# First transfers in another order, and the first norm's weights spread by TensorE

## The chip, the cores and the metric

The kernel runs on one core of one Trainium2 chip. The metric is the device time of one execution in microseconds (us), the median of several runs. The engines are named as the profile names them: PE is TensorE (matrix products), DVE is VectorE, ACT is ScalarE, POOL is GpSimd, SP is SyncE, which here only issues transfers (DMAs).

## The reference

One decoder layer over 1024 tokens of width 1024, all float32. What matters for this case is its first step; the rest is sketched.

```python
def rmsnorm(x, w):
    xf = x.astype(jnp.float32)
    y = xf * lax.rsqrt(jnp.mean(xf * xf, axis=-1, keepdims=True) + NORM_EPS)
    return (y * w.astype(jnp.float32)).astype(x.dtype)
...
    u = rmsnorm(h, norm1_w[l])                       # (1024, 1024), the first step
    proj = jnp.einsum('bsd,de->bse', u, w_in[l])     # 1024 x 3584
    ...
    ya = dilated_attention_group(qa, ka, va)         # 8 heads of 64, three window patterns
    yb = hgrn2_group(qb, fb, ib, gb, lb_table[l], hgrn_norm_w[l])   # 4 heads, gated recurrence
    h = h + jnp.einsum('bse,ed->bsd', mixed, w_out[l])
    u2 = rmsnorm(h, norm2_w[l])
    ...                                              # SwiGLU of width 2816, residual
    return rmsnorm(h, final_norm_w)
```

## The kernel before

The 1024 tokens are eight row tiles x0 to x7 of 128 rows, two to a buffer (`xb`, printed as `E`: x0 and x1, x2 and x3, and so on). Each tile goes through `norm_rows`: ACT squares it and sums each row (L337), DVE makes the mean (`msa`, L314), POOL raises it to the power -0.5 (`rsa`, L373), and DVE multiplies each half of 512 columns by `rsa` and by the norm's weights (L305, one SCALAR_TENSOR_TENSOR for each half). The weights `w1b` are two buffers of 128x512, `wh7` and `wl7`, in which each of the 128 rows holds the same 512 numbers: `norm1_w` is one row in memory, and a transfer with a step of zero (`bcast`) writes it 128 times.

Then `blocks` transposes the normed tile u on PE against the identity (`ident`, itself a transfer; four 128x128 transposes fill a bank `b` of PSUM, L286), and splits each bank into a rounded part (`hi`, ACT, L347) and a remainder (`lo`, DVE, L301), both fp32r, so that a product in full precision is three matmuls in fp32r: a triple. The input projection runs by a Strassen scheme: a 2x2 arrangement of blocks with seven products. Tiles 0 to 3 give the right operands 1 and 2 directly; for tiles 4 to 7 the first transpose is made by true fp32 matmuls with `ident` (L280), so that the sums of the scheme can be accumulated onto it. While the tiles come in, the first products of the scheme are begun with what is there ("leads": `F0` and `K1` in halves of 256 columns first, then two more in 512). The weights of each lead come through two staging buffers `st`.

After the projections the four recurrent heads (`hgrn`), the eight attention heads and the output projection follow. The attention stage takes a row maximum (`mx`, L1011), exponentials, transposes of the probabilities (L1048) and products; the output projection's matmuls stand between them where its inputs are ready. The feed-forward network takes the second half of the span.

What sets the order: the whole kernel is recorded as a list of operations (`P.op`, `P.flex`) with their dependencies, costs and a class `P.cls`. `Prog.schedule` then plays it through with these costs and takes, for each engine as it comes free, the ready operation of the lowest class, and within a class that with the longest way to the end. Operations recorded with `P.flex` can go to one of several engines (DVE, POOL, ACT), and the planner picks. Each engine works through its own list in the order so found, and waits where an operand is not ready. A changed dependency or cost anywhere can thus move instructions far behind it. All transfers are issued by SP, in its order, into one hardware queue. Constants that the recurrent heads need (`consts`: a mask `lm`, small tables `lg` and `hw`, an exponential on ACT) are recorded after the eighth tile, in the same class 2 as the rest.

Of the kernel before, what the change touches and what calls it, by code (L numbers as in the profile page):

```python
# [13 lines left out]
AF = mybir.ActivationFunctionType  # L14
# [5 lines left out]
S = 1024  # L20
D = 1024
# [225 lines left out]
def hymba_block(ctx: ExitStack, tc: tile.TileContext, x, norm1_w, w_in, lb_logits, hgrn_norm_w, w_out,  # L247
                norm2_w, w_gate_up, w_down, final_norm_w, cos, sin, amask, lmask, eye, out):
    nc = tc.nc
    x = x[0]  # L250
# [6 lines left out]
    P = Prog()  # L257
# [5 lines left out]
    def moved(nbytes, run):  # L263

        return nbytes / run * (0.008 + run / 27e3) / 16

    def dma(o, i, nbytes, run=2048):
        r = [i] if isinstance(i, (View, Buf)) else []
        w = [o] if isinstance(o, (View, Buf)) else []
        gi = i if r else (lambda: i)  # L270
        go = o if w else (lambda: o)
        P.op("SP", 0.5, lambda: nc.sync.dma_start(go(), gi()), r, w, nbytes=moved(nbytes, run))

    def mm(items, r, w):
        cost = sum(4 * n / 2400.0 + 0.008 if f32 else n / 2400.0 + (0.0132 if n > 128 else 0.007)
                   for o, lt, rh, st, sp, n, m, f32 in items)

        def fn():
            for o, lt, rh, st, sp, n, m, f32 in items:
                nc.tensor.matmul(o(), lt(), rh(), start=st, stop=sp, skip_group_check=True)  # L280
        P.op("PE", cost, fn, r, w)
# [73 lines left out]
    whole = lambda b: b.v(lambda t: t)  # L355

    def bcast(w, n):
        return bass.AP(tensor=w.tensor, offset=w.offset, ap=[[0, 128], [1, n]])


    ident = P.buf("ident", [128, 128])
# [15 lines left out]
    def norm_rows(xt, wb, o, scr, tag):  # L377
        ss = P.buf("ss" + tag, [128, 1])
        act(scr, xt, AF.Square, D, accum=whole(ss))
        r = rstd_of(ss, 1, D, tag)  # L380
        if not isinstance(wb, list):
            stt(o, xt, whole(r), wb, OP.mult, OP.mult, D)
            return
        for i, w in enumerate(wb):
            ov, xv = (v.buf.v(lambda b, v=v, i=i: v.get(b)[:, i * 512:i * 512 + 512], v.key + (i,)) for v in (o, xt))
            stt(ov, xv, whole(r), w, OP.mult, OP.mult, 512)
# [3 lines left out]
    def bank(stream, shape=(128, 512)):  # L390
        names = BANKS[stream]
        while True:
            n = rot[stream] = rot.get(stream, -1) + 1
            tag = f"b{names[n % len(names)]}"
            if tag not in held:
                return P.buf(tag, list(shape), F32, "ps")
# [25 lines left out]
    i_d = P.buf("i_d", [S, 512], F32, "dr")  # L422
    g_d = P.buf("g_d", [512, S], F32, "dr")
    f_d = P.buf("f_d", [512, S], F32, "dr")
    q_d = P.buf("q_d", [512, S], F32, "dr")
# [5 lines left out]
    def slot(tag):  # L431
        return whole(P.buf(tag, [128, 512]))
# [125 lines left out]
    def begin(R, w, rot, stream, p1, nw=8, cut=False):  # L558

        a = halves(True, w, rot)  # L560
        L = {}
        split(L, 1, a[0, 0], nw=nw, rot=rot, heng=LEADHI, leng=LEADLO)
        split(L, 2, a[0, 1], nw=nw, rot=rot, heng=LEADHI, leng=LEADLO)
        pa = bank(stream)
        held.add(pa.tag)
        if not cut:
            product(R, pa, L, 1, True, True)
            act(p1, whole(pa), AF.Copy, 512)
            product(R, pa, L, 2, False, True)
            yield pa, p1  # L570
            return
        for c in range(2):
            piece(R, pa, L, 1, True, True, c)
            act(colv(p1.buf, c * 256, 256, c),
                colv(pa, c * 256, 256, c), AF.Copy, 256)
            piece(R, pa, L, 2, False, True, c)
            yield pa, p1
# [49 lines left out]
    def consts():  # L627
        dma(lm, lmask, 128 * 640 * 4)
        for r in range(2):
            dma(tiny.v(lambda t, r=r: t[:, 4 * r:4 * r + 4]),  # L630
                bass.AP(tensor=lb_logits.tensor, offset=lb_logits.offset + r * 512, ap=[[1, 128], [128, 4]]), 2048)
        dma(hw, bass.AP(tensor=hgrn_norm_w.tensor, offset=hgrn_norm_w.offset, ap=[[1, 128], [128, 4]]), 2048)
        c = [tiny.v(lambda t, i=i: t[:, 4 * i:4 * i + 4]) for i in range(8)]
        tt("DVE", c[2], c[0], c[1], OP.max, 4)
        for r in range(2):
            tt("DVE", c[r], c[r], c[2], OP.subtract, 4)
        act(tiny.v(lambda t: t[:, 12:20]), tiny.v(lambda t: t[:, 0:8]), AF.Exp, 8)
        tt("DVE", c[2], c[3], c[4], OP.add, 4)
        P.op("DVE", 0.1, lambda: nc.vector.reciprocal(c[2](), c[2]()), [tiny], [tiny])
        tt("DVE", c[5], c[3], c[2], OP.mult, 4)  # L640
        ts("DVE", c[6], c[5], -1.0, 1.0, 4)
# [10 lines left out]
    def src_of(w):  # L652
        c = COL[w[0]] + int(w[1]) * 256
        return w_in_v[:, :, c:c + 256], w[0] in "QK"
# [3 lines left out]
    cut = []  # L658
    for t in range(NT):
        if t == 0:  # L660
            for i in range(4):
                dma(xs[i], x[i * 128:(i + 1) * 128, :], 128 * D * 4, 4096)
                if i == 0:
                    for k in range(2):
                        dma(w1b[k], bcast(norm1_w[:, k * 512:k * 512 + 512], 512), 128 * 512 * 4)
                    dma(ident, eye, 65536)
        if t == 2:
            for i in range(4, NT):
                dma(xs[i], x[i * 128:(i + 1) * 128, :], 128 * D * 4, 4096)
        xt = xs[t]  # L670
        u = us[t % 2]
        norm_rows(xt, w1b, u, u, "a")
        blocks(t, u, R, "n", tmp4)
        if t == 0:
            hi("ACT", whole(plus), whole(ident), 128)
            ts("POOL", whole(minus), whole(ident), -1.0, 0.0, 128)
        if t == 1:
            for w in seq[:CUT[0]]:
                cut.append(begin(R, *src_of(w), "d", slot(T8[4 + len(cut)]), 7, True))
                leads[w] = next(cut[-1])  # L680
        if t == 3:
            for g in cut:
                next(g)
        if t >= 3 and len(leads) < LEAD:
            w = seq[len(leads)]
            leads[w] = next(begin(R, *src_of(w), "d", slot(T8[4 + len(leads)]), 7))
    consts()

    csn = E(16, [128, 2048])
    for v, c0 in ((cos, 0), (sin, 1)):  # L690
# [133 lines left out]
    def hgrn(h):  # L824
# [16 lines left out]

        def blocked(v, w):
            return sub(v, lambda a: a.rearrange("p c (b e) -> p c b e", e=w))
        dma(f, f_d.v(lambda b: b[rs, :], h), 128 * S * 4)
        dma(qc(0, 128), q_d.v(lambda b: b[rs, :].rearrange("p (c e) -> p c e", e=128), h), 128 * S * 4, 512)
        dma(r128(iv), i_d.v(lambda b: b.rearrange("(c p) n -> p c n", p=128)[:, :, rs], h // 2), 128 * S * 4, 512)

        def scores(n, g):

# [87 lines left out]
                rd += [half(qp, c // 4), half(ks, (c - 1) // 4)]  # L937
            mm(it, rd, [o])
        gt = A
        dma(gt, g_d.v(lambda b: b[rs, :], h), 128 * S * 4)  # L940
        ss = P.buf("hss", [128, NT])
        for g in range(2):
            yg = half(iv, g)
# [435 lines left out]
```

## Time and profile before

| | us |
|---|---|
| median of 3 runs | 1258.24 (1257.98 to 1258.44) |
| profiled execution, its own time | 1256.03 |
| span of the profiled execution, first to last instruction | 1254.2 |
| PE busy within the span | 1212.3 |
| DVE busy | 1028.3 |
| ACT busy | 476.9 |
| POOL busy | 112.0 |

The page gives busy time, not need: PE is busy for 97% of the span, and 1254.2 - 1212.3 = 41.9 us are left in which it does nothing. The profiled execution is one run; it took 1256.03 us, 1.8 us more than its span, and 2.2 us less than the median.

The columns of the timeline are: start in us, duration in us, engine, line, operation, what it writes <- what it reads, its shape and count, and in brackets how long the engine had been idle before it and what it had waited for. Buffer numbers are left out, so `E` stands for many buffers.

### The profile page before, as it was taken

How to read it: one execution, taken by the hardware profiler on the slowest of the kernel's cores; microseconds unless marked ns; L12 is line 12 of the kernel's file. 1: busy time of each engine (PE TensorE's matmuls, PEld its weight loads, DVE VectorE, ACT ScalarE, POOL GpSimd, SP SyncE). 2: the span in 40 equal slices, each digit the busy share in tenths (PEclk: the TensorE clock that was granted, in tenths of full speed). 3: DMA queues.
4: the chain of work that ended last, by engine and by line, in shares of the span. 5: the costliest groups of instructions: out<-in, count | busy, mean ns of one | idle time of the engine just before them, and what ended most of it. 6: DMA issues, size and time to landing. Idle time of an engine off the chain costs nothing.

```text
span 1254.2 us, 17960 instructions
## 1 busy us (share of the span) xinstructions
PE 1212.3 (97%) x6244; PEld 1030.7 (82%) x6244; DVE 1028.3 (82%) x2110; ACT 476.9 (38%) x1020; POOL 112.0 (9%) x212
## 2 busy tenths in 40 slices
PE   4999999999998899999999999999999999999997
PEld 4878889888987788987888888888888887888885
DVE  6999989999789999966888676676676769968986
ACT  5642332344327887842722132221222223223222
POOL 1110000101003433420100000000000000000001
PEclk9999999999999999999999999999999999999998
DMA  8434443514468753316223322323322369434433
GB/s 264 133 127 160 176 147 101 182 68 160 132 195 272 203 143 88 93 54 199 79 76 126 118 97 89 126 85 109 126 84 101 112 230 386 170 101 127 135 109 118
DMA packets 132890, 175.57 MB, mean 140 GB/s; under 512 B 18496, under 2 KB 85696, under 8 KB 132800
## 3 DMA queue, kind: packets, MB, share of 16 engines
q1 hardware_dynamic: 132800, 174.43, 42.4%
q8 instruction: 49, 0.80, 0.3%
q14 instruction: 41, 0.34, 0.1%
HBM read 122.76 MB, written 51.64 MB: 139 GB/s over the span
## 4 chain that ended last, share of the span: by engine, by line
PE 78%; DVE 9%; DMA 7%; ACT 2%; issue 1%; SPq 0%; POOL 0%; DVEq 0%; POOLq 0%; ACTq 0%
PE b L280 76%; DVE wl L301 2%; DVE E L301 2%; PE b L1048 2%; DMA st<-in_w_in_dram 1%; DVE E L864 1%; DVE wh L301 1%; PE b L286 1%; DMA m_d<-lm 1%; DMA st<-in_w_out_dram 1%; DMA E<-kl_d 1%; DVE E L305 1%; DMA i_d<-wl 1%; DVE st L301 1%; ACT wh L337 1%
## 5 line engine op out<-in xcount | busy, mean ns | idle before, releaser
L280 PE MATMUL b<-E,wh 128*128 128x512 f32 (+1 forms) x2096 | 643.6, 389 | 5.1 <-ACT wl L337 1.9
L280 PEld LDWEIGHTS b<-E,wh 128*128 128x128 f32 x2096 | 386.3, 188 | 85.5 <-DVE E L301 4.0
L280 PE MATMUL b<-E,wl 128*128 128x512 f32 (+1 forms) x1048 | 403.9, 385 | 0.0
L347 ACT ACTIVATE wh<-st 128x512 fp32r<-128x512 f32 (+1 forms) x207 | 129.4, 629 | 384.6 <-PE b L280 217.1
L301 DVE TENSOR_TENSOR wl<-st,wh 128x512 fp32r<-128x512 f32 (+1 forms) x340 | 229.5, 685 | 5.3 <-ACT wh L347 2.1
L280 PEld LDWEIGHTS b<-E,wl 128*128 128x128 f32 x1048 | 197.1, 188 | 40.7
L301 DVE TENSOR_TENSOR E<-b,E 128x512 f32<-128x512 f32 (+1 forms) x157 | 105.5, 683 | 39.6 <-PE b L280 37.3
L349 DVE TENSOR_SCALAR wh<-st 128x512 fp32r<-128x512 f32 x119 | 50.0, 423 | 88.0 <-PE b L280 84.6
L280 PE MATMUL b<-wl,wh 128*128 128x512 f32 x308 | 119.9, 389 | 0.5 <-DVE wl L301 0.5
L280 PE MATMUL b<-wh,wl 128*128 128x512 f32 x308 | 119.9, 389 | 0.1
L280 PE MATMUL b<-wh,wh 128*128 128x512 f32 x308 | 119.8, 389 | 0.0
L280 PE MATMUL b<-wl,E 128*128 128x256 f32 (+1 forms) x544 | 116.3, 287 | 2.7 <-DVE wl L301 2.6
L301 DVE TENSOR_TENSOR wl<-b,wl 128x512 f32<-128x512 f32 (+2 forms) x139 | 89.6, 651 | 14.8 <-PE b L280 12.2
L280 PE MATMUL b<-E,E 128*128 128x192 f32 (+3 forms) x464 | 99.6, 324 | 2.0 <-DVE E L305 1.0
L301 DVE TENSOR_TENSOR st<-st 128x512 f32<-128x512 f32 x136 | 92.5, 684 | 0.7
L280 PEld LDWEIGHTS b<-wl,E 128*128 128x128 f32 x544 | 88.0, 191 | 5.8 <-DVE wl L301 3.4
L337 ACT ACTIVATE E<-E 128x512 f32<-128x512 f32 (+2 forms) x77 | 54.2, 704 | 93.5 <-DVE E L301 42.5
L280 PE MATMUL b<-wh,E 128*128 128x256 f32 x448 | 89.1, 290 | 0.2 <-DVE wh L301 0.2
L280 PEld LDWEIGHTS b<-E,E 128*128 128x128 f32 x464 | 75.0, 192 | 8.0 <-issue 2.6
L349 POOL TENSOR_SCALAR wh<-st 128x512 fp32r<-128x512 f32 (+1 forms) x16 | 11.1, 692 | 747.6 <-PE b L280 668.3
L280 PEld LDWEIGHTS b<-wh,E 128*128 128x128 f32 x448 | 72.4, 192 | 0.8 <-DVE wh L301 0.4
L280 PEld LDWEIGHTS b<-wl,wh 128*128 128x128 f32 x308 | 57.8, 188 | 13.0 <-DVE wl L301 0.9
(140 smaller groups left out, 1391.7 us busy)
## 6 DMA issues: line engine op xcount, KB each, us to landing
st<-in_w_gate_up_dram SPq DMA_DIRECT2D x22, 1024.0 KB, 5.2
st<-a_d SPq DMA_DIRECT2D x77, 256.0 KB, 2.8
st<-in_w_in_dram SPq DMA_DIRECT2D x16, 1024.0 KB, 5.7
a_d<-E SPq DMA_DIRECT2D x45, 256.0 KB, 2.1
E<-in_w_down_dram SPq DMA_DIRECT2D x44, 256.0 KB, 5.3
E<-in_x_dram SPq DMA_DIRECT2D x8, 512.0 KB, 9.1
E<-qs_d SPq DMA_DIRECT2D x32, 128.0 KB, 3.9
E<-kh_d SPq DMA_DIRECT2D x32, 128.0 KB, 3.6
```

What stands on the lines that cost most here:

```text
L280: nc.tensor.matmul(o(), lt(), rh(), start=st, stop=sp, skip_group_check=True)
L286: nc.tensor.transpose(ov(), iv(), ident())
L301: P.flex(alts, lambda e: ENG[e].tensor_tensor(o(), a(), b(), op=op), [a, b], [o])
L305: lambda e: nc.vector.scalar_tensor_tensor(o(), a(), s(), b(), op0=op0, op1=op1), [a, s, b], [o])
L337: nc.scalar.activation(o(), a(), func, **kw)
L347: nc.scalar.activation(o(), i(), AF.Copy)
L349: ENG[e].tensor_scalar(o(), i(), 1.0, 0.0, op0=OP.mult, op1=OP.add)
L864: nc.vector.copy_predicated(Av, mv, ps()[:, :, a:a + 64].rearrange("p c (b e) -> p c b e", e=w))
L1048: nc.tensor.transpose(ov(), iv(), ident())
```

## The change

The first transfers are issued in another order: x0, then two transfers of one row of 512 weights each (2 KB), then `ident`, and only then x1 to x3. The two broadcast transfers of 128x512 are gone. Instead, a row of ones (`ones`, 1x128, set by DVE) is multiplied with each weight row by one true fp32 matmul, which leaves the row 128 times in a PSUM bank. Tile x0's multiplication by the weights reads these banks (`w1p`); ACT copies the banks into `wh7` and `wl7` (`w1b`) for the other seven tiles. The steps up to x0's are in class 0, those after in class 2. `consts()` is recorded in class 3, so behind everything else that is ready. `dma` gets an argument for the queue; all its calls use SP, as before.

```diff
+        e = {"SP": nc.sync, "ACT": nc.scalar}[queue]
+        P.op(queue, 0.5, lambda: e.dma_start(go(), gi()), r, w, nbytes=moved(nbytes, run))
...
         if t == 0:
-            for i in range(4):
+            P.cls = 0
+            w1p = []
+            dma(xs[0], x[0:128, :], 128 * D * 4, 4096)
+            dma(ident, eye, 65536, 512)
+            rows = [P.buf(x, [1, 512]) for x in T8[:2]]
+            ones = P.buf("ones", [1, 128])
+            for k in range(2):
+                dma(rows[k], norm1_w[:, k * 512:k * 512 + 512], 2048)
+            P.op("DVE", 0.1, lambda: nc.vector.memset(ones(), 1.0), [], [ones])
+            for k in range(2):
+                ps = bank("d")
+                mm([(whole(ps), whole(ones), whole(rows[k]), True, True, 512, 128, True)], [ones, rows[k]], [ps])
+                P.cls = 2
+                act(w1b[k], whole(ps), AF.Copy, 512)
+                P.cls = 0
+                w1p.append(whole(ps))
+            P.cls = 2
+            for i in range(1, 4):
                 dma(xs[i], x[i * 128:(i + 1) * 128, :], 128 * D * 4, 4096)
-                if i == 0:
-                    for k in range(2):
-                        dma(w1b[k], bcast(norm1_w[:, k * 512:k * 512 + 512], 512), 128 * 512 * 4)
-                    dma(ident, eye, 65536)
...
-        norm_rows(xt, w1b, u, u, "a")
+        norm_rows(xt, w1b if t else w1p, u, u, "a")
...
+    P.cls = 3
     consts()
+    P.cls = 2
```

What the planner makes of it. On SP, at the start of the program (`E` holds x tiles, `st` the weights of the leads, first those of `K1`, 8x256 columns, then those of `F0`, 8x128), before:

```order
L272 DMA E_67<-in_x_dram 128x1024 x2
L272 DMA wh_70<-in_norm_w_dram 128x512
L272 DMA wl_72<-in_norm_w_dram 128x512
L272 DMA st_74<-in_w_in_dram 128x8x256
L272 DMA E_76<-in_x_dram 128x1024
L272 DMA ident<-in_eye_dram 128x128
L272 DMA st_80<-in_w_in_dram 128x8x128
L272 DMA E_76<-in_x_dram 128x1024
L272 DMA E_86<-in_x_dram 128x1024 x2
```

and after:

```order
L273 DMA E_67<-in_x_dram 128x1024
L273 DMA wh_71<-in_norm_w_dram 1x512
L273 DMA wh_73<-in_norm_w_dram 1x512
L273 DMA ident<-in_eye_dram 128x128
L273 DMA E_67<-in_x_dram 128x1024
L273 DMA E_78<-in_x_dram 128x1024
L273 DMA st_80<-in_w_in_dram 128x8x256
L273 DMA E_78<-in_x_dram 128x1024
L273 DMA E_86<-in_x_dram 128x1024
L273 DMA st_92<-in_w_in_dram 128x8x128
L273 DMA E_86<-in_x_dram 128x1024
```

The two weight rows and `ident` now stand right behind x0, and x1 and x2 ahead of the weights of `K1`; the weights of `F0` stand behind x3 and x4.

On PE, its first rows (`b` are PSUM banks; `ident,E` are transposes of u in L286, two rows to a tile; rows of three with 128x256 are a triple of a lead), before:

```order
L286 MATMUL b_122<-ident,E_83 128x128 x4
L286 MATMUL b_131<-ident,E_83 128x128 x4
L286 MATMUL b_142<-ident,E_83 128x128 x4
L286 MATMUL b_153<-ident,E_83 128x128 x4
L280 MATMUL b_176<-E_136,wh_138 128x256
L280 MATMUL b_176<-E_147,wh_138 128x256
L280 MATMUL b_176<-E_136,wl_151 128x256
L286 MATMUL b_189<-ident,E_83 128x128 x4
L286 MATMUL b_195<-ident,E_83 128x128 x4
L280 MATMUL b_176<-E_136,wh_138 128x256
```

and after:

```order
L281 MATMUL b_88<-wh_71,ones 128x512
L281 MATMUL b_103<-wh_73,ones 128x512
L287 MATMUL b_124<-ident,E_84 128x128 x4
L287 MATMUL b_130<-ident,E_84 128x128 x4
L287 MATMUL b_144<-ident,E_84 128x128 x4
L287 MATMUL b_153<-ident,E_84 128x128 x4
L287 MATMUL b_184<-ident,E_84 128x128 x4
L287 MATMUL b_191<-ident,E_84 128x128 x4
L281 MATMUL b_198<-E_136,wh_140 128x256
L281 MATMUL b_198<-E_138,wh_140 128x256
L281 MATMUL b_198<-E_136,wl_151 128x256
```

Two fp32 matmuls stand in front, the transposes of three tiles stand ahead of the first triple (before: of two tiles), and that triple is one of `K1` instead of `F0`. Rows that follow here are interleaved differently up to about row 190; then PE's order is the same for some 1495 rows, differs through the attention stage (rows 1685 to 2597 of 5610), and is the same for the last 3014. In the attention stage the output projection's first matmul stands at row 1865, before at row 1889.

On ACT, where the first sigmoid outputs of `F0` are made, the row of `lg` among them, before:

```order
L347 ACTIVATE E_352<-wh_476 128x4x128
L347 ACTIVATE wh_567<-st_312 128x512
L337 ACT_TABLE_LOAD
L337 ACTIVATE wh_573<-b_176 128x512
L337 ACTIVATE wl_595<-b_527 128x512
L347 ACTIVATE wh_651<-st_617 128x512
L337 ACTIVATE wh_639<-wh_639 128x512
L347 ACTIVATE E_398<-b_641 128x4x128
```

and after:

```order
L348 ACTIVATE E_337<-wh_456 128x4x128
L338 ACT_TABLE_LOAD
L338 ACTIVATE wh_562<-b_216 128x512
L348 ACTIVATE E_526<-b_570 128x4x128
L338 ACTIVATE wl_593<-b_516 128x512
L338 ACT_TABLE_LOAD
L338 ACTIVATE lg<-lg 128x8
L338 ACTIVATE E_681<-b_516 128x512
L338 ACT_TABLE_LOAD
L338 ACTIVATE wh_646<-wh_646 128x512
L338 ACTIVATE wh_583<-wh_583 128x512
```

Before, the exponential on `lg` stood in front, among the squares of the norm (as ACT's 27th row, behind tile x5). Now it stands between sigmoids, and ACT loads its function table for it and again for the sigmoids after it: 11 table loads in the program, before 9.

## Rows read from the trace of the kernel before

**Rows 1.** The page, its first part: busy us (share of span), instructions.

```profile
PE 1212.3 (97%) x6244; PEld 1030.7 (82%) x6244; DVE 1028.3 (82%) x2110; ACT 476.9 (38%) x1020; POOL 112.0 (9%) x212
```

**Rows 2.** Waits of PE: us in total, times, longest.

```profile
PE b L286 <- DMA ident<-in_eye_dram: 13.9, 1, 13.9
PE b L280 <- DVE mx L1011: 4.3, 3, 2.7
```

**Rows 3.** Windows of the span: busy us and instructions per engine, clock, DMA, GB/s.

```profile
core 0: us, PE busy (x) PEld busy (x) DVE busy (x) ACT busy (x) POOL busy (x), PEclk, DMA share, GB/s
0.00:14.00 14.00, 0.10 (x1) 0.13 (x2) 4.97 (x11) 4.43 (x7) 1.30 (x6) 1.00 0.82 271
14.00:20.00 6.00, 5.06 (x21) 4.37 (x22) 4.56 (x10) 4.76 (x10) 0.55 (x1) 1.00 1.04 402
20.00:30.00 10.00, 9.14 (x64) 8.59 (x63) 9.28 (x17) 6.42 (x13) 2.26 (x4) 1.00 0.76 205
30.00:40.00 10.00, 10.00 (x58) 8.54 (x57) 9.38 (x22) 7.94 (x17) 2.75 (x6) 1.00 0.60 198
...
350.00:400.00 50.00, 46.07 (x340) 43.59 (x341) 48.88 (x143) 24.78 (x70) 9.60 (x19) 1.00 0.70 225
400.00:450.00 50.00, 44.43 (x282) 38.29 (x281) 47.00 (x136) 38.52 (x105) 20.79 (x44) 0.97 0.63 179
```

**Rows 4.** Timeline, SP's first two issues: start, us.

```profile
0.72 0.87 SPq L272 DMA_DIRECT2D E<-in_x_dram  x2
```

**Rows 5.** DMA issues of 0 to 20 us, one kind: KB, us to landing.

```profile
lg<-in_lb_logits_dram SPq DMA_DIRECT2D x1, 2.0 KB, 8.6
```

**Rows 6.** Timeline, the first norm on ACT, POOL and DVE, and two splits.

```profile
4.47 1.06 ACT L337 ACTIVATE E<-E 128x1024 f32<-128x1024 f32 x1 [2.47 <-DMA E<-in_x_dram]
...
5.89 0.55 POOL L373 TENSOR_TENSOR rsa<-msa,mhalf 128x1 f32<-128x1 f32 x1 [5.46 <-DVE msa L314]
...
7.52 0.75 DVE L305 SCALAR_TENSOR_TENSOR E<-E,rsa,wh 128x512 f32<-128x512 f32 x1 [1.72 <-DMA wh<-in_norm_w_dram]
...
9.18 0.75 DVE L305 SCALAR_TENSOR_TENSOR E<-E,rsa,wl 128x512 f32<-128x512 f32 x1 [0.84 <-DMA wl<-in_norm_w_dram]
...
12.19 0.63 ACT L347 ACTIVATE wh<-st 128x512 fp32r<-128x512 f32 x1 [5.20 <-DMA st<-in_w_in_dram]
...
17.73 1.28 DVE L301 TENSOR_TENSOR E<-b,E 128x512 fp32r<-128x512 f32 x2
```

**Rows 7.** Timeline, PE's first work: transposes, triples of a product, fp32 products.

```profile
13.90 3.65 PE L286 MATMUL b<-ident,E 128*128 128x128 f32 x16 [13.90 <-DMA ident<-in_eye_dram]
...
18.22 0.58 PE L280 MATMUL b<-E,wh 128*128 128x256 f32 x1 [0.67 <-ACT E L347]
...
22.38 1.03 PE L286 MATMUL b<-ident,E 128*128 128x128 f32 x8
...
24.32 0.40 PE L280 MATMUL b<-E,wh 128*128 128x256 f32 x2
...
24.68 0.40 PE L280 MATMUL b<-E,wh 128*128 128x256 f32 x2
...
26.52 1.05 PE L280 MATMUL b<-ident,E 128*128 128x128 f32 x8
```

**Rows 8.** Timeline, ACT around its second table load.

```profile
54.39 1.28 ACT L337 ACT_TABLE_LOAD   x1
55.69 0.60 ACT L337 ACTIVATE wh<-b 128x512 f32<-128x512 f32 x1
...
64.26 0.63 ACT L347 ACTIVATE wh<-st 128x512 fp32r<-128x512 f32 x1 [4.40 <-DMA st<-in_w_in_dram]
```

**Rows 9.** Timeline, PE about PE's longest wait in the attention stage.

```profile
407.15 0.40 PE L280 MATMUL b<-E,E 128*128 128x512 f32 x1
410.23 0.50 PE L280 MATMUL b<-E 128*128 128x512 f32 x1 [2.68 <-DVE mx L1011]
...
411.19 0.63 PE L280 MATMUL b<-E,E 128*128 128x512 f32 x1
```

More of the change, by code (lines that the diff above doesn't have):

```diff
@@ L265, in moved, with dma @@
         return nbytes / run * (0.008 + run / 27e3) / 16
-    def dma(o, i, nbytes, run=2048):
+    def dma(o, i, nbytes, run=2048, queue="SP"):
         r = [i] if isinstance(i, (View, Buf)) else []
@@ L271, in dma @@
         go = o if w else (lambda: o)
-        P.op("SP", 0.5, lambda: nc.sync.dma_start(go(), gi()), r, w, nbytes=moved(nbytes, run))
+        e = {"SP": nc.sync, "ACT": nc.scalar}[queue]
+        P.op(queue, 0.5, lambda: e.dma_start(go(), gi()), r, w, nbytes=moved(nbytes, run))
     def mm(items, r, w):
@@ L843, in blocked @@
             return sub(v, lambda a: a.rearrange("p c (b e) -> p c b e", e=w))
-        dma(f, f_d.v(lambda b: b[rs, :], h), 128 * S * 4)
-        dma(qc(0, 128), q_d.v(lambda b: b[rs, :].rearrange("p (c e) -> p c e", e=128), h), 128 * S * 4, 512)
-        dma(r128(iv), i_d.v(lambda b: b.rearrange("(c p) n -> p c n", p=128)[:, :, rs], h // 2), 128 * S * 4, 512)
+        dma(f, f_d.v(lambda b: b[rs, :], h), 128 * S * 4, queue="SP")
+        dma(qc(0, 128), q_d.v(lambda b: b[rs, :].rearrange("p (c e) -> p c e", e=128), h), 128 * S * 4, 512, "SP")
+        dma(r128(iv), i_d.v(lambda b: b.rearrange("(c p) n -> p c n", p=128)[:, :, rs], h // 2), 128 * S * 4, 512, "SP")
         def scores(n, g):
@@ L939, in hgrn @@
         gt = A
-        dma(gt, g_d.v(lambda b: b[rs, :], h), 128 * S * 4)
+        dma(gt, g_d.v(lambda b: b[rs, :], h), 128 * S * 4, queue="SP")
         ss = P.buf("hss", [128, NT])
```

## The prediction

> **What bounds the kernel now.** I read the page's busy times first: PE does something in 1212.3 of 1254.2 us [rows 1], so only removing idle PE time, or time that PE spends at its lower clock, can shorten the run. The waits of PE say where the idle time is: 13.9 us stand in one piece at the start, before the first transpose, and the page puts them on `ident`; all other waits are small, the largest kind being the attention maximum `mx`, 4.3 us in three pieces [rows 2]. The windows show the same by stage. PE is idle for 13.9 of the first 14 us, for 0.94 of the next 6, for 0.86 of the next 10, then not at all to 40 us. In the attention stage 350 to 450 us it is idle for 3.93 + 5.57 = 9.5 us, with DVE busy for 48.88 and 47.00 of each 50 us [rows 3]. So there are two places: the start, which the change is about, and the attention stage, whose order it disturbs.
>
> The start is not bound by `ident` alone. PE's first 16 transposes take 3.65 us (0.23 each) and 8 later ones 1.03 us (0.13 each) [rows 7]: up to about 22 us PE runs at the lower of its two levels (1.2 against 2.4 GHz; the granted clock prints 1.00 over this stretch in rows 3, so I go by durations). And DVE is busy for 9.28 of the 10 us from 20 to 30 [rows 3]: from the moment the first transposes are there, the tile multiplications and remainders on DVE feed PE just in time. An earlier `ident` is worth only what DVE and ACT can follow.
>
> **The change part by part.** I follow the new order forward, with durations of before, until PE is filled again, and compare at a point where both have done the same work.
>
> Rows of the weights: SP issues x0 and x1 in 0.87 us, 0.44 each [rows 4], so the two weight rows go out at about 1.2 and 1.6 and `ident` at 2.0. They queue behind x0, whose square starts at 4.47 [rows 6]; I take 4.7 for their landing. No row shows a 2 KB transfer behind a single other one, so it is bounded. Early: x0 takes 4.47 - 0.72 = 3.75 us from issue to use, 1.3 of it for 512 KB at the 402 GB/s of a full queue [rows 3, 4, 6]; a transfer with almost nothing to move keeps 2.45, and lands at 3.7. Late: a 2 KB transfer of `lg` behind several MB took 8.6 us from issue [rows 5], which would be 9.8. 4.7 is nearest to x0's own landing, because just x0 is ahead. The Trainium skill ("DMA: Bandwidth & Descriptors", section "Anatomy of one DMA") gives a fixed cost of about 2 us for the GpSimd path; an estimate by it has the first row at 3.2 and, worked as below, a gain of 2.0 instead of 1.3; no run here shows so small a transfer alone.
>
> Two fp32 matmuls of 512 columns with one row of weights: an fp32 matmul of 128 columns takes 1.05 / 4 = 0.26 us at the higher level (its two records each make the x8) [rows 7], so 512 columns take 1.05, and at the lower level, by the ratio 0.23 / 0.13 of the transposes, 1.85. PE has them from 4.7 to 6.6 and to 8.4. They lie in the idle 13.9 us. x0's two multiplications ran at 7.52 and 9.18, each after its broadcast transfer [rows 6]. The first is now ready when `rsa` is (6.44 before, up to 7.1 with `plus` and `minus` put ahead of it on DVE), the second at 8.5 after the second product: u of x0 is complete at 9.3 instead of 9.93. So the products save 0.7 us over the broadcasts, and `ident` does the rest: the first transposes start at 9.4 instead of 13.90.
>
> The 4.5 us do not last. x1 now follows the rows and `ident`, lands about 6.1, is squared by 7.4; ACT copies the two banks for the other tiles (0.6 each, in its idle 5.20 us before 12.19 [rows 6]), and x1's u is done at 10.6. Its transposes run 11.2 to 13.0. Next late is `K1`: before, its weights were split at 12.19. The two broadcasts held the queue for about 9.18 - 7.52 = 1.66 us each [rows 6], at least 0.65 each at 402 GB/s [rows 3]; now x2 and `ident` are ahead, 0.59 MB or 1.46 us at that rate. So K1 lands between 12.19 - 3.3 + 1.46 = 10.3 and 12.19 - 1.3 + 1.46 = 12.4; I take the middle, 11.3. Behind that split ACT squares x2 (1.06 + 0.19, to 13.2) and rounds the second bank (to 13.8).
>
> From 13.8 DVE works without a break, in its new order: a remainder takes 1.28 / 2 = 0.64 [rows 6], the two multiplications of a tile 1.4, a small one 0.15, a split 0.43. Remainder, x2: 15.9. Mean, split of `F0`, remainder: 17.1. x3: 18.5. Two remainders of `F0`'s weights: 19.8. Mean and two remainders: 21.3. x4: 22.7. One remainder, which frees the bank for x4's first transposes: 23.3. PE in that time transposes x2 (16 to 17.8), runs the first triple at 17.8 (18.22 before), and is through with x4's fp32 transposes at 23.4 + 1.05 = 24.45. Before, these ended at 26.52 + 1.05 = 27.57 [rows 7]. By then the old order had run ten triples of 256 columns, the new one five; a triple takes 24.68 - 24.32 = 0.36 [rows 7], so 5 x 0.36 = 1.8 are still owed. **Head: 27.57 - 24.45 - 1.8 = 1.3 us gained.** Bounds: with K1 at 10.3 and rows at 3.7 about 2.8; with K1 at 12.4 about 0.2; with the rows at 9.8, a loss (below). From there PE is full in both orders [rows 3], so the lead is carried on.
>
> `consts` moved to class 3: the exponential on `lg` now stands among sigmoids and costs two more table loads, 1.28 us each, 1.30 to the next instruction (54.39 to 55.69), on ACT, which has an idle stretch of 4.40 us soon after [rows 8]. I cost them at nothing on the path; at worst the evacuation behind each is late and PE loses what its longest wait there allows, under 1.3. The Trainium skill ("ScalarE: Activation LUTs", section "What ACT_TABLE_LOAD costs") puts a switch at about 2.66 us, a drain included. Row 54.39 to 55.69 differs, and by the page ACT would still have most of its slack. `plus` going to DVE (0.22) and one split to POOL are inside the chain above.
>
> The attention stage: same instructions, another interleaving over some 900 of PE's rows, and a handful of small operations exchanged between DVE and POOL. I find no row that prices this; the nearest are its own waits. The longest is 2.68 us at 410.23, after which PE's records go from 0.40 to 0.63 for the same shape [rows 9], and the clock of that window is 0.97 of 50 us, so 1.5 us more [rows 3]. I take 0, because DVE, which is the scarcer engine there, has the same work; the bounds are one such wait less or more, 2.7 + 1.5 = 4.2 either way.
>
> Sum: 1256.03 - 1.3 = 1254.7 on the profiled execution's scale. That execution is 2.2 us under the median of the runs, so **1258.24 - 1.3 = 1256.9 us** for the median.
>
> **The rivals.** *A wait of the attention stage is filled.* The output projection's first matmuls stand 24 rows earlier on PE, which is what could run under a wait for `mx`. For: such waits are 4.3 us in all [rows 2]. Against: that wait comes before these matmuls even now. Time: 1256.9 - 2.7 = 1254.2, with the clock kept up as well 1252.7.
>
> *Slower: one more wait for `mx`.* Place: PE at 400 to 450 us, where DVE has 3 us of slack in 50 [rows 3]; the new order leaves PE once more with no projection work while DVE finishes a maximum. Price 2.7 + 1.5 = 4.2, and it decides once it is over the 1.3 gained plus the measurement's 2.5: 1256.9 + 4.2 = 1261.1.
>
> *The weight rows arrive no sooner than the large transfers.* At 9.8 the second product ends at 13.6, u of x0 at 14.4, and x1's multiplications (1.4) follow; PE starts 0.5 later than now and has one tile fewer ready: 1258.24 + 0.5 + 1.4 = 1260.1. Against: one transfer only is ahead of them.
>
> *The rows and K1 arrive early* (3.7 and 10.3): PE's products end 1.0 us sooner, of which half survives the wait for x1, and K1's split no longer holds up ACT: the 2.8 above, 1258.24 - 2.8 = 1255.4.
>
> **How the numbers follow.** About 0.2% (2.5 us) is what a measurement of this kernel can tell from no change, so faster is under 1255.7 and slower over 1260.8. Forecast as it stands 0.43; a filled wait 0.27; early rows and K1 0.07; one more wait 0.16; late rows 0.07. Faster: 0.27 + 0.07 and 0.03 of the forecast's own spread, 0.37. Slower: 0.16 and 0.02 of the late rows, 0.18. The rest, 0.45, is no difference. The range takes in the filled wait with its clock and the added wait: 1252.5 to 1261.3.
>
> **What would show it.** In the trace after: the two products end by 8.5 and transposes start by 9.5; PE idle again 13 to 16; first triple about 17.8; from 24 us PE full; at 50 us PE is one to two us further in the same rows. At 54 to 70 us two more loads on ACT without a PE wait behind them. In 350 to 450 us idle PE time near 9.5. Wrong would be: weight rows landing after 7; PE never idle between 13 and 24, a gain of 3 or more; a changed idle sum in 350 to 450 that outweighs the start.

## The result

The changed kernel takes **1268.11 us** (median of 5 runs, 1264.11 to 1269.04) against 1257.98 us of the kernel before on the same chip: ratio of the means 1.0075, 95% interval 1.0052 to 1.0098. So it is slower, by 0.75%; forecast were 1256.9 us, with 1261.3 as the upper end of the range. The profiled execution took 1269.04 us, with a span of 1267.3 us.

The head of the program went much as forecast. The timeline of PE after, first rows (start, duration, engine, line, operation, and in brackets idle time and releaser):

```profile
4.70 3.75 PE L281 MATMUL b<-wh,ones 1*128 1x512 f32 x4 [4.70 <-DMA wh<-in_norm_w_dram]
8.37 1.11 PE L287 MATMUL b<-ident,E 128*128 128x128 f32 x4
10.17 1.11 PE L287 MATMUL b<-ident,E 128*128 128x128 f32 x4 [0.68 <-DVE E L306]
...
17.79 0.78 PE L281 MATMUL b<-E,wh 128*128 128x256 f32 x2
...
22.30 1.13 PE L281 MATMUL b<-ident,E 128*128 128x128 f32 x8
```

The weight rows are there at 4.70, the two products end at 8.45, the first transposes start at 8.37 where they stood at 13.90 [rows 7], the first triple at 17.79, and x4's fp32 transposes end at 23.43, which was 27.57 [rows 7].

The windows after (columns: busy us and instructions of PE, PEld, DVE, ACT, POOL, granted clock, DMA share, GB/s), to be held against [rows 3]:

```profile
0.00:14.00 14.00, 8.03 (x20) 4.02 (x20) 5.49 (x13) 7.66 (x13) 1.92 (x7) 1.00 0.86 291
...
350.00:400.00 50.00, 44.43 (x314) 41.78 (x314) 45.45 (x131) 21.14 (x56) 10.53 (x17) 0.96 0.60 190
400.00:450.00 50.00, 45.41 (x271) 39.83 (x272) 44.90 (x135) 35.25 (x99) 18.48 (x38) 0.90 0.60 185
```

In 350 to 450 us PE idles for 5.57 + 4.59 = 10.2 us, where it was 9.5, but the granted clock is 0.96 and 0.90, where it was 1.00 and 0.97.

Where the time went is best read from the **lead**: the start of a matmul in the profiled execution of before, minus the start of the same matmul here, matched along PE's stream. After is 1.0 us ahead at 60 us and 1.2 at 120 and 200; 0.9 behind at 355, 7.2 behind at 545, 13.0 behind at 1240. A second execution of before (before_again, below) differs from the first by up to 1.3 us in this, and executions of the same instructions with only the buffers moved by up to 3.0 (pad_before and all_by_32, below). So the small steps are within the spread and two are not: **6.3 us are lost between 355 and 545 us** (attention), and **5.9 us between 545 and 1240 us** (feed-forward network, FFN), where nothing was forecast to happen. PE's waits there are the same few in both kernels, 3.6 us in all before and 3.9 after, and from 700 to 1000 us it has none. Windows of PE in that part, before (busy us and number of matmuls touched, clock, DMA share, GB/s):

```profile
700.00:800.00 100.00, 100.00 (x441) 1.00 0.28 98
800.00:900.00 100.00, 100.00 (x442) 1.00 0.28 98
900.00:1000.00 100.00, 100.00 (x441) 1.00 0.30 105
```

and after:

```profile
700.00:800.00 100.00, 100.00 (x437) 1.00 0.30 102
800.00:900.00 100.00, 100.00 (x437) 1.00 0.31 106
900.00:1000.00 100.00, 100.00 (x436) 1.00 0.29 100
```

PE is busy throughout, at the full clock, and gets four or five matmuls fewer through in each 100 us. From the starts of the matmuls the mean interval is 227.6 ns before and 229.8 ns after (700 to 1000 us). The order of the instructions there is the same.

### The profile page after: what moved, and what is told of

The parts are those of the page before. It is cut to its first block, busy times and chain, and to the rows that moved or that the text cites. A ratio compares the mean times of both kernels' runs of the same rounds, so it can differ in the third digit from the quotient of the medians.

```text
span 1267.3 us, 17961 instructions
## 1 busy us (share of the span) xinstructions
PE 1226.0 (97%) x6248; PEld 1034.7 (82%) x6248; DVE 1032.9 (82%) x2122; ACT 478.7 (38%) x1016; POOL 114.5 (9%) x209
## 4 chain that ended last, share of the span: by engine, by line
PE 79%; DVE 12%; DMA 5%; ACT 2%; issue 1%; POOL 1%; SPq 0%; POOLq 0%; DVEq 0%; ACTq 0%
PE b L281 76%; DVE E L302 3%; DVE wl L302 2%; PE b L1064 2%; DVE E L880 1%; DVE E L306 1%; DVE wh L1027 1%; DMA E<-kl_d 1%; PE b L287 1%; DMA st<-in_w_out_dram 1%; DVE E L889 1%; DMA st<-in_w_gate_up_dram 1%; DMA v_d<-wl 1%; DMA i_d<-wl 1%; DVE wh L302 1%
## 5 line engine op out<-in xcount | busy, mean ns | idle before, releaser
L281 PE MATMUL b<-E,E 128*128 128x192 f32 (+4 forms) x464 | 99.4, 324 | 5.4 <-DVE E L306 3.7
```

## Experiments

Each kernel was timed beside the kernel before. Ratios are to before, with a 95% interval; "interval" is the mean time from matmul to matmul in 700 to 1000 us; leads are taken against the profiled execution of before, as above.

### The bank counter

The two weight products take their PSUM banks from the rotation `bank("d")`, five banks in turn, which all projection products use. They leave it two banks further on, so every later projection product waits for the evacuation of another bank than before, and the planner, which sees that, interleaves differently. *rot_back* is the kernel after with the counter set back:

```diff
                 w1p.append(whole(ps))
+            rot["d"] = -1
             P.cls = 2
```

PE then has the order of before from 55 us on, and every engine from some 150 us on. *shift_before* is the converse, the kernel before with the counter two banks on (`rot["d"] = 1` ahead of the first projection product): it has the order of after, on PE from 58 us on and on every engine from some 150 us on.

> The changed kernel, with the rotation of PSUM banks set back after the two weight products, so that every later product of the projection has the bank that it has in the kernel before; from about 90 us on every engine then has the order of before. Theory A (the two products draw two banks, all later projection products shift by two of five, and with the banks the planner's order of the attention stage changes): the attention stage is as long as before (PE idle near 9.5 us in 350 to 450 us), the start's lead is kept, 1255 to 1258 us. Theory B (the new start itself, its transfers or TensorE's clock, costs the time): no change against the changed kernel, 1264 to 1268 us. Theory C (another placement of buffers in SBUF slows every matmul a little): between, about 1262 us, since the placement is still another than before.

> The kernel before, unchanged but for the rotation of PSUM banks advanced by two before the projection; transfers and weights as before. Theory A: the attention stage takes the changed kernel's order and loses 6 to 8 us there, 1263 to 1268 us. Theory B: 1258 us, as before. Theory C: somewhere above 1258, with longer intervals from matmul to matmul in the feed-forward stage.

With them ran both kernels once more, *after_again* and *before_again*:

> The changed kernel once more, for the spread between executions: its five runs lay at 1264.1, 1264.2 and at 1268.1 to 1269.0. Theories A and B: the attention stage again loses 6 to 7 us against before. If the second loss, 5.8 us from 620 us to the end with the same order of instructions, belongs to the kernel, it is there again; if it belongs to the execution, a run near 1264 us shows it at 1 to 2 us.

> The kernel before once more, for the spread between executions: 1255 to 1258.5 us. Its intervals from matmul to matmul between 700 and 1000 us were 227.6 ns in the profiled execution; the changed kernel's 229.6 to 230.1. If that belongs to the execution, this run may show either.

Measured: rot_back 1258.45 us, 1.0023 (1.0010 to 1.0035); shift_before 1258.69, 1.0028 (1.0015 to 1.0041); after_again 1266.1, 1.0084 (1.0066 to 1.0103); before_again 1255.96, 1.0002 (0.9990 to 1.0015).

Had the order been all of it (theory A), rot_back would be back at before's time or under it and shift_before at after's, 1263 us or more. Each stands a third of the way: there are two causes. Between 355 and 545 us shift_before loses 7.9 us and rot_back nothing; between 545 and 1240 us rot_back loses 4.8 and shift_before nothing (a gain of 0.4). after_again loses 3.7 us in the first stretch, less than the 6 to 7 expected, and 5.2 in the second. The order of the attention stage hangs on the counter. The slower FFN does not: interval 229.9 ns in rot_back, 227.6 in shift_before.

### 512 bytes

What else is different behind 545 us? `ones` is one more buffer, of 512 bytes per partition, ahead of all others, and PE's stream is two matmuls longer. The PSUM banks are no suspect there: the last 3130 matmuls, from 542 us on, have the same operands and the same banks in before and after. *pad_before* puts an unused buffer of that size in front, in the kernel before (`P.buf("pad", [1, 128])()`). *rot_fit* and *after_fit* put `ones` into a buffer that exists anyway (`wh10`, which thereby comes first in SBUF), rot_fit with the counter set back as well:

```diff
-            ones = P.buf("ones", [1, 128])
+            ones = P.buf(T8[2], [1, 128])
```

*pe_only* is rot_fit with the transfers in the old order: x1 ahead of the weight rows, `ident` behind x3.

> The kernel before with one unused buffer of [1, 128] allocated ahead of everything, so that each buffer in SBUF lies 512 bytes further on; the instructions, their order and the PSUM banks are those of before. Theory P (placement: the matmuls from 620 us on are slower because their operands lie 512 bytes further on): mean interval from matmul to matmul in 700 to 1000 us 229.5 to 230.2 ns as in the kernel after, where before has 227.6 to 227.8, the first 600 us unchanged, total +4.5 us (+0.36%). Rival I (instruction stream or PSUM banks): interval 227.6 to 227.8 ns, total as before within 0.1%.

> The kernel after with two edits: the bank counter is set back after the two weight products, and the vector of ones lies in a buffer that a later weight tile uses anyway, so that the FFN's operands lie at the same place modulo 1024 bytes as in before. Order from 90 us on as before; PSUM banks and the instruction stream as in after. Theory P (placement): interval 227.6 to 227.8 ns, the head's lead of 1.9 us is kept to the end, total -1.9 us (-0.15%; -0.05 to -0.25%). Rival I (instruction stream or PSUM banks): interval 229.5 to 230.2 ns, total +0.2 to +0.3% as the run with the counter set back alone.

> The kernel after with the vector of ones in a buffer that a later weight tile uses anyway (FFN operands at the same place modulo 1024 bytes as in before), the bank counter left as the change leaves it, so the attention stage keeps the order of after. Theory P with order: interval 227.6 to 227.8 ns from 620 us on, but 2 to 7 us lost between 360 and 542 us; total +0.1 to +0.5%, and some 5 us under after. Rival I: interval 229.5 to 230.2 ns, total +0.84% as after.

> Products of TensorE for the weights, but x1 ahead of their rows and ident last as in before; counter set back and the ones in an existing buffer. Order from 40 us on as before. If the head's gain comes from the early ident: the first transposes start at 13.9 us as in before, x0's norm ends some 2 us sooner with nobody to use it, lead at 115 us 0 to 0.5 us, total within 0.1% of before. If it comes from the weight rows: lead 1 to 2 us, total -0.1 to -0.15%.

Measured: pad_before 1256.68 us, 1.0005 (0.9994 to 1.0015), interval 227.6; rot_fit 1259.29, 1.0025 (1.0015 to 1.0034), 229.9; after_fit 1266.46, 1.0078 (1.0063 to 1.0093), 229.8; pe_only 1260.43, 1.0030 (1.0017 to 1.0042), 229.9.

Theory P fell: 512 bytes do nothing (pad_before), and taking them away mends nothing. pe_only was expected within 0.1% of before and stands 0.30% over it, with the slow interval of the others. The intervals, sorted by operand, told more (from the start of a matmul to the start of the next, mean over 700 to 1000 us). In before all FFN matmuls take 226 to 227 ns but those of one product of seven, which reads `E14` and `E7`. PE's timeline of before shows such a product of twelve matmuls, and the product read from other buffers just ahead of it:

```profile
809.82 0.62 PE L280 MATMUL b<-E,wh 128*128 128x512 f32 x2
...
812.54 0.62 PE L280 MATMUL b<-E,wh 128*128 128x512 f32 x2
...
813.90 0.63 PE L280 MATMUL b<-E,wh 128*128 128x512 f32 x2
...
816.70 0.62 PE L280 MATMUL b<-E,wh 128*128 128x512 f32 x2
```

812.54 - 809.82 = 2.72 us for the fast one, 816.70 - 813.90 = 2.80 for the slow one. `E14` starts at a multiple of 64 bytes, all other operands of the FFN start 32 bytes past one. In the kernel after two more large buffers lie at a multiple (byte in a partition, from the built programs, remainder by 64 in brackets):

```
          mhalf       E0          wh7         E14         other operands of the FFN
before    16512 (0)   16544 (32)  24736 (32)  62144 (0)   (32)
after     25216 (0)   17024 (0)   82304 (0)   54464 (0)   (32)
```

Buffers are laid out in the order of their first use. Before, the 32 bytes of `mhalf` came first and pushed `E0`, the buffer of x0 and x1, off the multiple. With x0's transfer now ahead of everything, `E0` comes first; and `wh7`, no longer the target of an early transfer, moved behind other buffers. The small `plus` and `minus` are at a multiple too. In the three kernels with `ones` in `wh10` (rot_fit, after_fit, pe_only) `wh10` is at a multiple as well. Of the last 3130 matmuls, 176 have one operand at a multiple and the other 32 past in before, 583 in after, 691 in rot_fit. In rot_fit, matmuls of `E14` with `wh` weights take 234.0 ns where the weights lie 32 past, and 225.5 (eight matmuls) where they are in `wh7`, at a multiple like `E14`. So the suspicion: a matmul is slow where its two operands start in different halves of 64 bytes.

### Halves of 64 bytes

Four kernels, in which buffers are only laid out otherwise, by naming them before the first instruction. *e0_moved*, before with `E0` ahead of `mhalf`:

```diff
+    P.buf("E0", [128, 2048])()
     with tc.manual_schedule():
```

*all_by_32*, before with 32 unused bytes in front (`P.buf("pad", [1, 8])()`). *rot_halves*, rot_fit with

```diff
+    P.buf("mhalf", [128, 8])()
+    P.buf("wh7", [128, 4, 128])()
     with tc.manual_schedule():
```

and *e14_moved*, before with `mhalf` and `E14` named first.

> The kernel before with the buffer E0 allocated ahead of the 32-byte buffer mhalf and not behind it, as it comes out in the kernel after: E0 starts at a multiple of 64 bytes, all other buffers, banks, instructions and their order are as in before. Theory M (a matmul is slow when its two operands start at different halves of 64 bytes: one at a multiple of 64, the other 32 past one; in the traces E14, at a multiple of 64, with weights 32 past takes 235.3 and 232.8 ns in before, and 225.5 where the weights too lie at a multiple): E0 and E1's product slow, mean interval 700 to 1000 us 228.3 to 229.8 ns (before 227.6), total +1.5 to +4.5 us (+0.12 to +0.36%). Rival I (two more matmuls in TensorE's stream, or PSUM banks): interval 227.6 ns, total within 0.1% of before.

> The kernel before with one unused buffer of 32 bytes ahead of everything: every buffer 32 bytes further on, so that nearly all operands of the FFN start at a multiple of 64 bytes, and E14 alone 32 past one. Theory M (only different halves cost): product 4 with E14 stays the slow one, mean interval 227.6 ns as before, total within 0.1%. Rival N (a multiple of 64 is slow as such): six of seven products slow, interval 232 to 233 ns, total +10 to +13 us (+0.8 to +1.0%). Rival I: as before.

> The kernel after with the bank counter set back, the ones in a buffer that exists anyway, and mhalf and wh7 allocated first, so that E0 and wh7 start 32 bytes past a multiple of 64 as all other operands of the FFN but E14 do. PSUM banks and TensorE's stream as in after. Theory M: mean interval 227.6 ns (after 229.6 to 230.1), the head's lead of 1.7 to 2.1 us is kept to the end, total -1.9 us (-0.05 to -0.25%). Rival I (stream or banks): interval 229.5 to 230.1 ns, total +0.2 to +0.3%.

> The kernel before with mhalf and E14 allocated first: E14 starts 32 bytes past a multiple of 64 as the other operands of the FFN do; all else as in before. Theory M: the twelve matmuls of the product that reads E14 and E7, 232 to 235 ns each in before, fall to 227; that is one product of seven: interval 226.7 ns for 227.6, total -2 to -3 us (-0.16 to -0.24%). Rival I, and any theory in which that product is slow for another reason (VectorE idle beside it, its turn): product stays at 232 to 235, total within 0.1%.

Measured: e0_moved 1259.52 us, 1.0023 (1.0007 to 1.0040), interval 229.3; all_by_32 1256.6, 1.0005 (0.9988 to 1.0023), 227.6; rot_halves 1253.19, 0.9971 (0.9958 to 0.9985), 227.6; e14_moved 1254.86, 0.9991 (0.9976 to 1.0007), 226.7.

Theory M held in all four intervals. The time of rot_halves is under the expected range (-0.05 to -0.25%), and its head is 3.0 us ahead at 60 us, for 1.7 to 2.1. With `E0` alone moved, its matmuls with `wh` and with `wl` weights take 233.1 and 230.3 ns where they took 226.5 and 227.0. With everything moved by 32 bytes nothing changes, so a multiple of 64 is not slow as such; there `E14`, now 32 past one, is still the slow one, at 235.2 and 232.5. With `E14` in line with the others its matmuls take 226.9 and 226.2. A window of e14_moved, all engines (PE, PEld, DVE, ACT, POOL, clock, DMA share, GB/s):

```profile
700.00:800.00 100.00, 100.00 (x443) 82.81 (x442) 67.84 (x116) 23.69 (x41) 0.00 (x0) 1.00 0.28 98
```

443 matmuls in 100 us, for 441 before and 437 after. In total e14_moved gains 1.6 us from 545 to 1240 us, less than the 2 to 3 expected; its ratio is not told from 1.

### The order alone, the transfers alone, and the best

*after_halves* is the kernel after with `mhalf` and `wh7` named first, so the order of after without the halves. *dma_only* is the kernel before with only the transfers reordered, and no products:

```diff
-            for i in range(4):
+            P.cls = 0
+            dma(xs[0], x[0:128, :], 128 * D * 4, 4096)
+            dma(ident, eye, 65536, 512)
+            for k in range(2):
+                dma(w1b[k], bcast(norm1_w[:, k * 512:k * 512 + 512], 512), 128 * 512 * 4)
+            P.cls = 2
+            for i in range(1, 4):
                 dma(xs[i], x[i * 128:(i + 1) * 128, :], 128 * D * 4, 4096)
```

(the old transfers of weights and identity go out). *best_of_both* is rot_halves with `E14` named first as well.

> The kernel after with mhalf and wh7 allocated first, so that E0 and wh7 start 32 bytes past a multiple of 64; the bank counter, and with it the attention stage's order, stay as in after. If the two causes add: mean interval 700 to 1000 us 227.6 ns, lead over before 1 to 3 us up to 360 us, 5 to 9 us lost between 360 and 542 us, flat behind; total +3 to +7 us (+0.25 to +0.55%), which is 4.5 to 5.5 us under after. If the halves were all of it: total -0.1 to -0.25%.

> The kernel before with the first transfers reordered alone (x0, identity, the two broadcast weight transfers, x1 to x3), no products. Order from 542 us on as in before, halves as in before. The broadcast weights still land after x0; if the early identity and rows are what the head's lead comes from: first transposes at 9 to 11 us for 13.9, lead at 115 us 1.5 to 2 us, as with the whole change. If it takes the products too (weights in PSUM at 6.6 and 8.4 us, no 512 KB of broadcast in front of x1): lead 0 to 1 us, as the products alone had 0.2 us. Interval 227.6 ns by either.

> The kernel after with the bank counter set back, the ones in a buffer that exists anyway, and mhalf, wh7 and E14 allocated first, so that all operands of the FFN start 32 bytes past a multiple of 64. If the gains add: interval 226.7 ns, lead over before 2 to 3 us at 360 us and 2 to 3 us more from 620 us to the end, total -4 to -6 us (-0.3 to -0.5%). If not (the end is bound elsewhere): -0.2 to -0.3% as rot_halves.

(In the text on dma_only, "from 542 us on" is a slip: PE has the order of before from 51 us on, and every engine from 127 us on.)

Measured: after_halves 1260.69 us, 1.0034 (1.0015 to 1.0052), interval 227.6; dma_only 1253.51, 0.9980 (0.9965 to 0.9995), 227.6; best_of_both 1251.54, 0.9958 (0.9941 to 0.9976), 226.7.

The two causes add, roughly. With the halves of before, the order costs 1.0034 - 0.9971 = 0.63% behind the new head (after_halves against rot_halves), but only 0.28% behind the old one (shift_before against before). Part of that difference is the head itself: at 60 us rot_halves is 3.0 us ahead, after_halves 0.6. The halves cost 1.0075 - 1.0034 = 0.41% with the order of after, and 1.0023 - 0.9971 = 0.52% with that of before (rot_back against rot_halves). These ratios come from several chips, each against the kernel before on the same chip.

By stretch, change of the lead in us, grouped by what each kernel has:

```
                                          355 to 545    545 to 1240
order of after, halves mixed
  after / after_again / after_fit    -6.3 / -3.7 / -4.0    -5.9 / -5.2 / -8.1
order of after, halves as in before
  after_halves / shift_before        -6.0 / -7.9           -1.2 / +0.4
order of before, halves mixed
  rot_back / rot_fit / pe_only        0.0 / +1.1 / -0.8    -4.8 / -5.8 / -5.7
  e0_moved (E0 alone)                +0.2                  -2.6
order of before, halves as in before
  before_again / pad_before          +1.4 / +2.0           +0.6 / -0.1
  all_by_32 / dma_only / rot_halves  -1.6 / -1.8 / +0.2    +0.5 / +0.5 / -0.1
order of before, E14 in line too
  e14_moved / best_of_both           -0.4 / +0.4           +1.6 / +2.2
```

All five traces with the order of after lose 3.7 to 7.9 us in the attention stage; the eleven others lie between -1.8 and +2.0. The traces of after and shift_before, with the two largest losses, are the slowest executions of their series. after_fit, rot_fit and pe_only have the mixed `wh10` besides in the second stretch.

One thing that the order changes shows at 396 us. PE's timeline after:

```profile
397.06 0.40 PE L281 MATMUL b<-E,E 128*128 128x512 f32 x1
400.94 1.22 PE L281 MATMUL b<-wl,E 128*128 128x256 f32 x4 [3.48 <-ACT E L338]
```

PE stands for 3.48 us before a product of the output projection, for an operand that ACT writes (`E<-b,rsh`, the scaled recurrent heads). That wait, of 3.47 to 3.49 us, is in all five traces with the order of after and in none of the twelve with that of before; eleven of these twelve have one of 1.7 us for DVE (`wl`, L301) before such a product. Windows of after about it (PE busy, clock, DMA share, GB/s):

```profile
396.00:399.00 3.00, 1.21 (x4) 1.00 0.97 295
399.00:402.00 3.00, 1.06 (x5) 0.55 1.02 406
402.00:405.00 3.00, 3.00 (x16) 0.50 0.82 269
405.00:408.00 3.00, 2.72 (x19) 0.81 1.00 366
```

The granted clock falls to 0.50 behind the wait, that is to the level of 1.2 GHz, and is at 0.81 in the last window; before falls as low in one window of 3 us only, behind its wait for `mx` [rows 9]:

```profile
411.00:414.00 3.00, 3.00 (x13) 0.52 0.89 352
```

Counted over 350 to 545 us, idle PE time plus lost clock is 11.1 us before (idle 3.93 + 5.57 + 0.11, clock 0.03 x 50) and 18.6 after (idle 5.57 + 4.59 + 1.43, clock (0.04 + 0.10) x 50): 7.5 more, against 6.3 lost in the lead. In this pair only 2 of the 7.5 are idle time, but the other executions differ. Counted the same way:

```
                                        idle PE time       lost clock
order of after, five traces       10.7 to 12.0, mean 11.5    3.0 to 7.0, mean 5.2
order of before, twelve traces     7.3 to 12.2, mean  9.1    1.5 to 4.0, mean 2.3
```

So on average the order costs 2.4 us of idle time and 2.9 us of clock. That it comes from the one wait at 396 us is not shown: no run removed that wait alone.

On the head: with the order and halves of before, the whole change (rot_halves, best_of_both) is 3.0 and 3.2 us ahead at 120 us, the transfers alone (dma_only) 2.3, the products alone (pe_only) 0.5. In dma_only the planner issues both broadcasts ahead of the identity, and x1 behind all three. The broadcasts land at 6.54 and 7.23 us, before at 7.38 and 9.15, and the identity at 7.43, before at 13.76. Its DVE timeline:

```profile
7.45 0.23 DVE L314 TENSOR_SCALAR minus<-ident 128x128 fp32r<-128x128 f32 x1 [1.70 <-DMA ident<-in_eye_dram]
7.59 0.75 DVE L305 SCALAR_TENSOR_TENSOR E<-E,rsa,wh 128x512 f32<-128x512 f32 x1
8.26 0.75 DVE L305 SCALAR_TENSOR_TENSOR E<-E,rsa,wl 128x512 f32<-128x512 f32 x1
```

Both multiplications follow without a wait for `wh` or `wl`, and PE starts at 8.44, earlier than the 9 to 11 expected. So the new order of the transfers brings most of the gain; which part of it is the identity's and which the broadcasts', no run separates. What the products add, 0.9971 against 0.9980, is within the intervals.

## Why the prediction was wrong

**The weight rows at 4.7: right.** 4.70, and the products end at 8.45 for 8.4. The estimate by the Trainium skill ("DMA: Bandwidth & Descriptors", section "Anatomy of one DMA", whose figure is for the GpSimd path), 3.2, was too early: SP issues both rows between 1.17 and 1.77, so the first took up to 3.5 us with x0 ahead of it.

**The head's chain: right in its course, its size in part by luck.** First transposes 8.4 for 9.4 (I had u of x0 in one piece; PE begins with its first half, and DVE multiplied at 6.85), K1's split 11.49 for 11.3, first triple 17.79 for 17.8, x4's transposes 23.43 for 24.45. Two terms were late: x1 landed at 7.13 for 6.1, and u of x0 was complete at 10.12 for 9.3. There DVE stood until ACT's copy of the second bank had ended:

```profile
9.37 0.75 DVE L306 SCALAR_TENSOR_TENSOR E<-E,rsa,b 128x512 f32<-128x512 f32 x1 [0.82 <-ACT wl L338]
```

By my own sum the measured end of x4's transposes would give 27.57 - 23.43 - 1.8 = 2.3 us. The lead at 60 us is 1.0 in after and 0.3 to 1.3 in after_again, after_fit and after_halves: 1.3 us are gone again in after by then, of which PE's idle time explains some 0.6 (1.2 us from 23.43 to 60 us, and 0.6 from 27.57 in before). So the forecast of 1.3 came near because x4's transposes were early by about what was lost behind them. With the counter set back the lead is 2.7 to 3.1, so the size depends on the order behind it.

**`consts` in class 3: wrong attribution, right cost.** Two more table loads stand at 55.10 and 66.50 after, and no wait of PE stands behind them. But dma_only, where `consts` keeps class 2, has them too (55.65 and 65.50), and rot_halves, with class 3, has none. shift_before, with the counter two on, has none either. Their place comes from the planner's order in the head, not from the class or the counter alone. A load takes 1.28 us and ACT's next instruction starts 1.29 behind its start:

```profile
55.10 1.28 ACT L338 ACT_TABLE_LOAD   x1
56.39 0.21 ACT L338 ACTIVATE lg<-lg 128x8 f32<-128x8 f32 x1
```

The row agrees with the trace of before [rows 8]. The Trainium skill ("ScalarE: Activation LUTs", section "What ACT_TABLE_LOAD costs") has the same 1.28 us for the load, and 2.66 us with a drain; the trace shows no such drain behind the load.

**The attention stage at 0: the step that failed first.** I saw that the order changed there and found no row to price it, took 0, and bounded it by one `mx` wait and its clock, 4.2 us. The order has 3.7 to 7.9. The rival "one more wait for `mx`" had the right place and the right kind of mechanism; but the wait that is new is for ACT's heads, and the clock lost over 350 to 545 us is on average 2.9 us more than with the order of before, not 1.5. The sign of being wrong that I named, the idle sum of 350 to 450 us, hardly shows it: 10.2 us for 9.5. I also took the reason for the reordering from the head in general; it is the two banks, a part of the change that I didn't cost at all.

**"From there PE is full in both orders, so the lead is carried on": the step that failed second.** There was no term for a stage whose instructions and order are unchanged. The FFN lost 5.9 us there, because two buffers, `E0` and `wh7`, moved into the other half of 64 bytes: with both put back (after_halves) the stretch loses 1.2 us and the interval is that of before. A row to suspect it by was in the trace of before: the product that took 2.80 us beside others of 2.72.

The sum with both in place, from after's lead: +1.0 at 60 us, -1.8 to 355, -6.3 to 545, -5.9 to the end, together -13.0, which is the 1269.04 - 1256.03 us of the two profiled executions. The medians differ by 10.1, and the profiled after_again (1263.12 us) is 7.1 behind at 1240. (The 1.8 up to 355 us are the least certain term: after_again, after_fit and after_halves gain 1.4 to 2.6 in that stretch.)

## What to carry to other kernels

An edit at the start of a planned kernel has two side doors to its far end: shared counters (here a bank rotation) that move the plan, and the layout of buffers by first use. Print both for before and after, and set them back, before costing anything else. Where PE is saturated, look at the time from matmul to matmul, not at its busy share: it was 100% in the fast and in the slow kernel. Here the change's own gain was real: with the order, `E0` and `wh7` put back it is 0.29% faster than before (0.15 to 0.42%), and 0.42% (0.24 to 0.59%) with `E14` in line with them, which the kernel before could have had as well.

## What the runs showed of the hardware

A matmul of 128x512 (fp32r) is followed by the next after 226 to 227 ns where its two operands and those around it start in the same half of 64 bytes (e14_moved, mean 226.7). One whose operands are mixed, one at a multiple of 64 and the other 32 bytes past one, takes 230 to 235 ns on average. Which of the two halves they share makes no difference: 227.0 ns for 1190 matmuls with both 32 past in before, and for 1190 with both at a multiple in all_by_32.

Matmuls that are not mixed slow down too when mixed ones are near. `E7`, which lies like its weights, took 232 ns between matmuls of `E14`, and 226.9 once `E14` was in line. It is not the next one alone: in e0_moved two such matmuls, at 827.90 and 828.59 us, take 236 ns, four and seven places behind the last mixed one. In after, from 700 to 1000 us, 329 mixed matmuls take 232.8 ns on average and the 976 others 228.8, where e14_moved has 226.7; so about half of the loss lies in matmuls that are not mixed themselves.

Why is open: no run read one operand alone, and none tried distances other than 32. The Trainium skill ("SBUF — State Buffer", section "Operand start alignment") asks only that an operand start at a multiple of its element size, and says that this is about legality and not speed. All operands here do, and the time still differs.
